# Two edits in the first front of a two-layer decoder trunk: the pace of the U gathers, and an output projection in plain f32

## The chip, the cores and the metric

One core of one Trainium2 chip runs the whole program. The time is device time of one execution in microseconds (us); the kernel before took 3003.43 us, the median of three runs (2999.48 to 3004.02). Everything is float32 in and out.

## The reference

The input is 512 tokens of 1024 features. Layer 0 mixes tokens by attention, layer 1 by a gated convolution, and each is followed by an expert retrieval (PEER):

```
for i in range(2):
    h = rmsnorm(x, norm_mix[i])
    x = x + (attention(h) if i == 0 else short_gated_conv(h))
    h = rmsnorm(x, norm_ffn[i])
    x = x + peer_ffn(h, w_query[i], sub_keys[i], u[i], v[i])
```

The attention has 16 query heads and 4 key heads of 64, a window of 128 keys, a sink per head, and ends in the output projection `o @ w_o` (1024 x 1024). The PEER step scores 2 x 128 sub-keys in each of 8 heads, takes the best 16 of the pairs per head, and so gives each token 128 of 16384 experts: `a = u[idx] . x`, `w = softmax(g) * gelu(a)`, `y = sum w * v[idx]`.

## The kernel before, in words

The tokens are four tiles of 128. The expert step is done in two ways. For tiles 2 and 3 it is **dense** (`dense`): all 16384 experts pass in 128 steps of 128 rows; each step streams one 512 KB piece of U (transposed) and one of V from HBM, splits both into a high and a low float32r part, and multiplies three products of them. For tiles 0 and 1 it is **gathered** (`gather`): 128 indirect DMAs by POOL fetch one U row per token each (`ug`, line 631, 512 KB each), VectorE multiplies each with the normed token and sums it (line 634); after the last, ScalarE's gelu and VectorE make the weights, which TensorE transposes, and 128 further gathers fetch V rows (`vg`, line 662), which TensorE multiplies in pairs (line 672). The gathered tiles share six buffers of the tag `gat`. Tile 0 and tile 1 of layer 0 follow one another in this chain, then tile 0 and tile 1 of layer 1: 1024 gathers in all.

Three generators are merged into one program order (`merge`). `stream_d` goes through the stages: attention and router of tile 0, then the **first front** (attention of tiles 1 to 3 and their router), the dense stage of layer 0, a second front (convolution of tiles 1 to 3 and their router), the dense stage of layer 1. `stream_g` is the chain of gathers, `stream_f` the small steps of tiles 0 and 1 in between. Each `yield` gives a length in the planner's own units, and the stream with the smallest sum goes on. In the first front the QKV part has 12 yields of 3.0 for all three tiles, the attention 4 yields of 6.0 per tile, the projection 8 of 10.5, the router of tiles 1 to 3 another 133 units: 36 + 72 + 84 + 133 = 325. `stream_g` waits after each gather for `rate()`: 1.3 units during the router of tile 0, and in the first front `FR0`, whose first number is for U gathers and whose second is for V gathers; in the dense stage 2.4.

```
def rate():
    u = 0 if st.get("gu") else 1
    if st["dense"]:
        return (DR1 if "f1" in st else DR0)[u]
    if st["front"]:
        return (FR1 if "f0" in st else FR0)[u]
    return GR0
```

This order is not that of the instructions in the engines' queues. A planner goes over the program with a timeline of its own and lets each engine take the earliest in program order of what it holds ready; work that is due later fills time that it takes to be free. The V matmuls are put earlier by a number of instructions: 3000 when they come up in a front, 600 otherwise. Each engine then works through its own queue in order.

The **output projection** is `proj` (line 181 on), called at the end of `attn` and of `conv`. For each half of the columns it loads four pieces of the weights (`wpo`, tag `w`, four buffers, line 186), and for each tile multiplies two 128-row slices per piece into a PSUM bank per tile (tag `y`, four banks). With `sp` given, each piece is first split: ScalarE casts it to float32r (`woh`, line 191), VectorE subtracts (`wol`, line 192), and three matmuls replace one: high x high, high x low, low x high (lines 198 to 200). The splits of the attention lie in the tag `sc` (four buffers), which the score tiles of the softmax use as well. The attention output is split in the same way (`oTh` line 342, `oTl` line 344). Without `sp`, one f32 matmul is issued (line 202); tile 0, whose attention is run alone, has always had this form.

Of the kernel before, what the change touches and what calls it, by code (L numbers as in the profile page):

```python
# [8 lines left out]
F32 = mybir.dt.float32  # L9
F32R = mybir.dt.float32r  # L10
# [5 lines left out]
ALU = mybir.AluOpType  # L16
# [3 lines left out]
P = 128  # L20
# [22 lines left out]
SCB = 4  # L43
# [27 lines left out]
P3 = 1  # L71
# [3 lines left out]

DR0 = (2.4, 2.4)
DR1 = (2.5, 2.5)
FR0 = (3.0, 3.0)
FR1 = (3.0, 3.0)


# [1 line left out]
def trunk(ctx: ExitStack, tc: tile.TileContext, a: dict, out: bass.AP):  # L83
    nc = tc.nc
# [39 lines left out]
    def py(name="py"):  # L124
        return ps_y.tile([P, 512], F32, name=name, tag="y")
# [7 lines left out]
    def pmm(name="pm"):  # L133
        return ps_m.tile([P, 512], F32, name=name, tag="m")

    def rstd_of(dst, ss, n):
        nc.vector.tensor_scalar(dst, ss, 1.0 / n, EPS, op0=ALU.mult, op1=ALU.add)
        nc.scalar.activation(dst, dst, AF.Sqrt)
        nc.vector.reciprocal(dst, dst)
# [105 lines left out]
    def attn(tiles, qks, pool, L):  # L245
        n = len(tiles)
        kT, vs, qkg, sink, nsink, cos, sin, mask = L
        nh = NH + NKV
        oTs = []
        sp = P3 and n > 1  # L250
        for j, t in enumerate(tiles):
            qk = qks[j]
            sq = pool.tile([P, nh, HD], F32, name="qsq", tag="qsq")
            nc.scalar.activation(sq, qk, AF.Square)
            ss = s2.tile([P, nh], F32, name="qss")
            nc.vector.tensor_reduce(ss, sq, axis=AX.X, op=ALU.add)
            r = s2.tile([P, nh], F32, name="qr")
            rstd_of(r, ss, HD)
            nc.vector.tensor_tensor(qk, qk, r.unsqueeze(2).to_broadcast([P, nh, HD]), op=ALU.mult)
            nc.vector.tensor_tensor(qk, qk, qkg, op=ALU.mult)  # L260
            cb = cos[:, t:t + 1, :].to_broadcast([P, nh, RH])
            sbb = sin[:, t:t + 1, :].to_broadcast([P, nh, RH])
            x1 = qk[:, :, 0:RH]
            x2 = qk[:, :, RH:2 * RH]
            rt = pool.tile([P, 4, nh, RH], F32, name="rt", tag="qsq")
            nc.vector.tensor_tensor(rt[:, 0], x1, cb, op=ALU.mult)
            nc.vector.tensor_tensor(rt[:, 1], x2, sbb, op=ALU.mult)
            nc.vector.tensor_tensor(rt[:, 2], x2, cb, op=ALU.mult)
            nc.vector.tensor_tensor(rt[:, 3], x1, sbb, op=ALU.mult)
            nc.vector.tensor_tensor(x1, rt[:, 0], rt[:, 1], op=ALU.subtract)  # L270
            nc.vector.tensor_tensor(x2, rt[:, 2], rt[:, 3], op=ALU.add)
            kd = pool.tile([P, NKV, 2, HD], F32, name="kd", tag="kd")
            nc.scalar.copy(kd, qk[:, NH:, :].unsqueeze(2).to_broadcast([P, NKV, 2, HD]))
            ps = py("psk")
            for g in range(NKV):
                nc.tensor.transpose(ps[:, g * P:(g + 1) * P], kd[:, g].rearrange("p a d -> p (a d)"), ident)
            nc.scalar.copy(kT[:, :, t * P:(t + 1) * P], ps.rearrange("p (g t) -> p g t", g=NKV))
            qT = pool.tile([P, KC, P], F32, name="qT", tag="qT")
            for half in range(2):
                ps = py("psqT")  # L280
                for k in range(4):
                    hp = half * 4 + k
                    nc.tensor.transpose(ps[:, k * P:(k + 1) * P],
                                        qk[:, 2 * hp:2 * hp + 2, :].rearrange("p a d -> p (a d)"), ident)
                nc.scalar.copy(qT[:, half * 4:half * 4 + 4, :], ps.rearrange("p (k t) -> p k t", k=4))
            if sp:
                oT = pool.tile([P, 2, 4, P], F32R, name="oTh", tag="hTa", bufs=4)
                oL = pool.tile([P, 2, 4, P], F32R, name="oTl", tag="qk", bufs=3)
            else:
                oT = oL = pool.tile([P, 2, 4, P], F32, name="oT", tag="hTa", bufs=4)  # L290
            oTs.append([(lambda k, o=o: o[:, k // 4, k % 4, :]) for o in (oT, oL)])
            if t == 0:
                k0, kw, moff, blks = 0, P, P, [0]
            else:
                k0, kw, moff, blks = (t - 1) * P, 2 * P, 0, [t - 1, t]
            nb = len(blks)
            for gp2 in range(2):
                pso = (pa, pf)[gp2]("pso")
                for gh in range(2):
                    g = gp2 * 2 + gh  # L300
                    sc = pool.tile([P, 4, 2 * P], F32, name="sc", tag="sc", bufs=SCB)
                    scv = sc[:, :, :kw]
                    psc = [py(f"psc{q}") for q in range(2)]
                    for rr in range(2):
                        for par in range(2):
                            lo = par * 64
                            nc.tensor.matmul(psc[par][:, rr * kw:(rr + 1) * kw],
                                             qT[lo:lo + 64, 2 * g + rr, :],
                                             kT[lo:lo + 64, g, k0:k0 + kw], start=True, stop=True)
                    mb = mask[:, moff:moff + kw]  # L310
                    m = s2.tile([P, 4], F32, name="m", bufs=4)
                    for r4 in range(4):
                        nc.vector.tensor_tensor_reduce(out=scv[:, r4], in0=psc[r4 % 2][:, (r4 // 2) * kw:(r4 // 2 + 1) * kw],
                                                       in1=mb, scale=0.125, scalar=GONE, op0=ALU.add, op1=ALU.max,
                                                       accum_out=m[:, r4:r4 + 1])
                    sk = sink[:, 4 * g:4 * g + 4]
                    nm = s2.tile([P, 4], F32, name="nm", bufs=4)
                    nc.vector.scalar_tensor_tensor(nm, m, -1.0, nsink[:, 4 * g:4 * g + 4],
                                                   op0=ALU.mult, op1=ALU.min)
                    es = s2.tile([P, 4], F32, name="es", bufs=4)  # L320
                    nc.vector.tensor_tensor(es, sk, nm, op=ALU.add)
                    nc.scalar.activation(es, es, AF.Exp)
                    den = s2.tile([P, 4], F32, name="den", bufs=4)
                    for r4 in range(4):
                        nc.scalar.activation(scv[:, r4], scv[:, r4], AF.Exp, bias=nm[:, r4:r4 + 1],
                                             accum_out=den[:, r4:r4 + 1])
                    nc.vector.tensor_tensor(den, den, es, op=ALU.add)
                    nc.vector.reciprocal(den, den)
                    for r4 in range(4):
                        nc.scalar.mul(scv[:, r4], scv[:, r4], den[:, r4:r4 + 1])  # L330
                    for b in range(nb):
                        psp = pmm("psp")
                        for r4 in range(4):
                            nc.tensor.transpose(psp[:, r4 * P:(r4 + 1) * P],
                                                scv[:, r4, b * P:(b + 1) * P], ident)
                        pT = pool.tile([P, 512], F32, name="pT", tag="pT", bufs=2)
                        nc.scalar.copy(pT, psp)
                        nc.tensor.matmul(pso[gh * 64:gh * 64 + 64, :], vs[:, blks[b], g * HD:(g + 1) * HD], pT,
                                         start=(b == 0), stop=(b == nb - 1))
                    yield 6.0  # L340
                psov = pso.rearrange("p (r q) -> p r q", r=4)
                nc.scalar.copy(oT[:, gp2], psov)
                if sp:
                    nc.vector.tensor_tensor(oL[:, gp2], psov, oT[:, gp2], op=ALU.subtract)
        for t in tiles:
            xs[t] = pool.tile([P, D], F32, name="x", tag="x", bufs=3)
            nc.sync.dma_start(xs[t], a["x"][t * P:(t + 1) * P, :])
        yield from proj(a["wo"], oTs, tiles, py, (pool, ("sc", "sc"), SCB) if sp else None)

    def conv(tiles, pool, psum, slow=1.0):  # L350
        n = len(tiles)
# [450 lines left out]
    def rate():  # L802
# [3 lines left out]
# [3 lines that stand above are left out]
# [179 lines left out]
```

## Time and profile before

| | |
|---|---|
| median of three runs | 3003.43 us (2999.48 to 3004.02) |
| the profiled execution | 2992.02 us |
| its span, first to last instruction | 2990.3 us |
| TensorE busy | 2626.9 us, 88% |
| VectorE busy | 2235.7 us, 75% |
| ScalarE busy | 1559.1 us, 52% |
| POOL busy | 1365.3 us, 46% |
| bytes moved | 931.38 MB, mean 311 GB/s |
| mean granted TensorE clock | 0.947 of full speed |

In the profile PE is TensorE's matmuls, PEld its weight loads, DVE VectorE, ACT ScalarE, SP the engine that issues plain DMAs. L634 is line 634 of the kernel. A name such as `ug<-in_u_dram,idx` gives the tile written and the tensors read. Times in the rows are from the span's start. The ends of matmuls are modelled and overlap, so the cost of one is read from start to start. A plain f32 matmul leaves two records, an fp32r one leaves one.

### The profile page before, as it was taken

To read this page: it belongs to the slowest core of one execution; us is meant where nothing else is said; L and a number is where in the kernel's file an instruction comes from. 1 tells how busy PE (TensorE), PEld (TensorE's weight loads), DVE (VectorE), ACT (ScalarE), POOL (GpSimd) and SP (SyncE) were. 2 spreads that over 40 slices of the span, in tenths; PEclk is the share of its full clock that TensorE was granted. 3 is DMA by queue.
4 is the path that set the end of the run, shared out by engine and by line. 5 is a ranking of instruction groups with operands and counts; after the bars stand their busy time and mean duration, and the time that the engine had idled before them with its cause. 6 is when DMAs were issued, how large, how long until landed. Compare 5 with 4: busy or idle time off the path is not lost. (4 is left out here: it accounts for less than half of the span.)

```text
span 2990.3 us, 53463 instructions
## 1 busy us (share of the span) xinstructions
PE 2626.9 (88%) x19980; PEld 2083.9 (70%) x19980; DVE 2235.7 (75%) x5234; ACT 1559.1 (52%) x2384; POOL 1365.3 (46%) x1154
## 2 busy tenths in 40 slices
PE   5974699869999889999998689997888699999998
PEld 5762368636988767777787686773677577777897
DVE  2499849888998987446699774899899957446554
ACT  4224533685673458348444333358466449547543
POOL 0157733366344455534467424236566755554000
PEclk8986799989999999999999799997999899999999
DMA  5888988989999988998999867789999998998554
GB/s 199 283 315 306 341 293 276 329 308 382 365 353 389 323 318 290 345 328 291 363 408 396 310 220 279 249 319 318 363 349 360 345 359 297 333 317 302 192 189 157
DMA packets 263204, 931.38 MB, mean 311 GB/s; under 512 B 29984, under 2 KB 38560, under 8 KB 262944
## 3 DMA queue, kind: packets, MB, share of 16 engines
q0 software_dynamic: 147456, 536.94, 49.5%
q1 hardware_dynamic: 115488, 391.03, 36.3%
q8 instruction: 157, 2.57, 0.3%
q14 instruction: 103, 0.84, 0.1%
HBM read 916.31 MB, written 11.53 MB: 310 GB/s over the span
## 5 line engine op out<-in xcount | busy, mean ns | idle before, releaser
L631 POOL DMA_INDIRECT ug<-in_u_dram,idx x512 | 668.3, 1305 | 638.1 <-DVE act L634 312.5
L662 POOL DMA_INDIRECT vg<-in_v_dram,idxT x512 | 572.2, 1118 | 689.1 <-PE acc L672 571.7
L634 DVE CUSTOM_DVE_ANT_0 ug<-ug,xn 128x1024 f32<-128x1024 f32 x512 | 622.8, 1226 | 40.3 <-DMA ug<-in_u_dram,idx 39.3
L176 PE MATMUL psA<-xh,uh 128*128 128x256 f32 x2048 | 521.1, 292 | 46.0 <-ACT uh L696 19.0
L177 PE MATMUL psA<-xl,uh 128*128 128x256 f32 x2048 | 504.2, 284 | 0.0
L176 PEld LDWEIGHTS psA<-xh,uh 128*128 128x128 f32 x2048 | 391.1, 191 | 127.9 <-ACT wh L719 32.7
L697 DVE TENSOR_TENSOR ul<-du,uh 128x1024 fp32r<-128x1024 f32 x256 | 316.6, 1237 | 181.0 <-ACT uh L696 179.1
L697 DVE TENSOR_TENSOR vl<-dv,vh 128x1024 fp32r<-128x1024 f32 x256 | 316.2, 1235 | 145.2 <-ACT vh L696 121.8
L177 PEld LDWEIGHTS psA<-xl,uh 128*128 128x128 f32 x2048 | 392.0, 191 | 4.5 <-issue 0.5
L696 ACT CAST uh<-du 128x1024 fp32r<-128x1024 f32 x256 | 268.6, 1049 | 205.3 <-PE psA L177 172.6
L696 ACT CAST vh<-dv 128x1024 fp32r<-128x1024 f32 x256 | 268.5, 1050 | 162.7 <-PE y L731 139.7
L672 PE MATMUL acc<-vg,wd 128*32 128x512 f32 x2048 | 318.1, 635 | 31.4 <-DMA vg<-in_v_dram,idxT 30.9
L731 PE MATMUL y<-vh,wh 128*128 128x512 f32 x1024 | 290.2, 406 | 34.9 <-ACT vh L696 29.9
L179 PE MATMUL psA<-xh,ul 128*128 128x256 f32 x2048 | 288.7, 283 | 10.1 <-DVE ul L697 10.0
L731 PE MATMUL y<-vl,wh 128*128 128x512 f32 x1024 | 285.7, 401 | 12.8 <-DVE vl L697 12.8
L731 PE MATMUL y<-vh,wl 128*128 128x512 f32 x1024 | 285.5, 399 | 3.0 <-DVE wl L720 3.0
L179 PEld LDWEIGHTS psA<-xh,ul 128*128 128x128 f32 x2048 | 261.8, 189 | 21.8 <-DVE ul L697 16.6
L738 ACT COPY jr<-ijg 128x2048 f16<-128x2048 f16 x128 | 243.2, 1900 | 35.0 <-DVE oj L742 33.1
L731 PEld LDWEIGHTS y<-vh,wh 128*128 128x128 f32 x1024 | 179.4, 191 | 86.5 <-ACT vh L696 36.7
L731 PEld LDWEIGHTS y<-vl,wh 128*128 128x128 f32 x1024 | 190.1, 191 | 62.9 <-DVE vl L697 18.8
L731 PEld LDWEIGHTS y<-vh,wl 128*128 128x128 f32 x1024 | 194.8, 192 | 50.9 <-DVE wl L720 4.7
L742 DVE TENSOR_TENSOR oj<-jr,io 128x2048 f16<-128x2048 f16 x128 | 157.4, 1229 | 78.0 <-PE psG L751 66.7
(208 smaller groups left out, 4021.1 us busy)
## 6 DMA issues: line engine op xcount, KB each, us to landing
du<-in_uT_dram SPq DMA_DIRECT2D x256, 512.0 KB, 6.6
dv<-in_v_dram SPq DMA_DIRECT2D x256, 512.0 KB, 5.9
wpc<-in_wq_dram SPq DMA_DIRECT2D x64, 512.0 KB, 4.8
wpc<-in_w_in_dram SPq DMA_DIRECT2D x48, 512.0 KB, 5.9
wpo<-in_wo_dram SPq DMA_DIRECT2D x16, 512.0 KB, 7.5
ug<-in_u_dram,idx POOLq DMA_INDIRECT x512
vg<-in_v_dram,idxT POOLq DMA_INDIRECT x512
wpo<-in_w_out_dram SPq DMA_DIRECT2D x16, 512.0 KB, 5.2
```

Source lines behind the costliest of these rows:

```text
L176: nc.tensor.matmul(ps, w[0][:, k, :], x[0][:, k, ts], start=(k == 0), stop=False)
L177: nc.tensor.matmul(ps, w[0][:, k, :], x[1][:, k, ts], start=False, stop=False)
L179: nc.tensor.matmul(ps, w[1][:, k, :], x[0][:, k, ts], start=False, stop=(k == KC - 1))
L631: nc.gpsimd.indirect_dma_start(out=ug, out_offset=None, in_=a[f"u{l}"], in_offset=bass.IndirectOffsetOnAxis(ap=r["idx"][h][:, c:c + 1], ax ...
L634: nc.vector.tensor_tensor_reduce(out=ug, in0=ug, in1=xn, scale=1.0, scalar=0.0, op0=ALU.mult, op1=ALU.add, accum_out=act[:, s:s + 1])
L662: ld = nc.gpsimd.indirect_dma_start(out=vg, out_offset=None, in_=a[f"v{l}"], in_offset=bass.IndirectOffsetOnAxis(ap=idxT[:, tt:tt + 1], ax ...
L672: mm = nc.tensor.matmul(acc[c:c + 32, :], wd[:, j, r8, :], vgs[j][:, h * 512:(h + 1) * 512], start=(q == 0 and r8 == 0), stop=(q == 3 and ...
L696: nc.scalar.copy(hi, w)
L697: nc.vector.tensor_tensor(lo, w, hi, op=ALU.subtract)
L731: nc.tensor.matmul(ys[tt][h], x[:, tt * P:(tt + 1) * P], m[:, h * 512:(h + 1) * 512], start=first and k == 0, stop=last and k == len(terms ...
L738: nc.scalar.copy(jr, ijg[:, 0, t0:t0 + TG].unsqueeze(2).to_broadcast([P, TG, P]))
L742: nc.vector.tensor_tensor(oj, jr, io128.unsqueeze(1).to_broadcast([P, TG, P]), op=ALU.is_equal)
```

## The change

`FR0`, the pace of the gathers in the first front, goes from 3.0 to 6.0 for U gathers and stays at 3.0 for V gathers. `attn` no longer splits anything: for tiles 1 to 3, too, the attention output is one f32 tile, and `proj` is called without `sp`. The split in `proj` stays for the convolution.

```
-FR0 = (3.0, 3.0)
+FR0 = (6.0, 3.0)
...
-        sp = P3 and n > 1
...
-            if sp:
-                oT = pool.tile([P, 2, 4, P], F32R, name="oTh", tag="hTa", bufs=4)
-                oL = pool.tile([P, 2, 4, P], F32R, name="oTl", tag="qk", bufs=3)
-            else:
-                oT = oL = pool.tile([P, 2, 4, P], F32, name="oT", tag="hTa", bufs=4)
-            oTs.append([(lambda k, o=o: o[:, k // 4, k % 4, :]) for o in (oT, oL)])
+            oT = pool.tile([P, 2, 4, P], F32, name="oT", tag="hTa", bufs=4)
+            oTs.append([lambda k, o=oT: o[:, k // 4, k % 4, :]])
...
                 nc.scalar.copy(oT[:, gp2], psov)
-                if sp:
-                    nc.vector.tensor_tensor(oL[:, gp2], psov, oT[:, gp2], op=ALU.subtract)
...
-        yield from proj(a["wo"], oTs, tiles, py, (pool, ("sc", "sc"), SCB) if sp else None)
+        yield from proj(a["wo"], oTs, tiles, py, None)
```

## Rows read from the trace of the kernel before

**Rows 1.** The page, busy tenths in 40 slices of 74.8 us each.

```profile
PE   5974699869999889999998689997888699999998
DVE  2499849888998987446699774899899957446554
```

**Rows 2.** Stretches: us; busy of PE, PEld, DVE, ACT, POOL; clock, DMA share, GB/s.

```profile
220.00:260.00 40.00, 14.45 (x48) 10.17 (x48) 38.88 (x103) 16.64 (x52) 28.36 (x24) 0.54 0.88 302
260.00:300.00 40.00, 20.87 (x88) 10.54 (x88) 39.49 (x102) 23.31 (x61) 28.89 (x24) 0.76 0.88 306
300.00:340.00 40.00, 22.14 (x92) 10.74 (x92) 38.07 (x104) 22.76 (x67) 30.23 (x25) 0.80 0.92 326
340.00:372.00 32.00, 24.68 (x76) 11.39 (x77) 27.03 (x49) 16.16 (x32) 24.07 (x20) 0.76 0.98 360
372.00:405.00 33.00, 33.00 (x166) 22.50 (x164) 11.15 (x14) 7.05 (x9) 11.49 (x12) 1.00 0.81 292
...
420.00:665.00 245.00, 208.69 (x1954) 154.80 (x1956) 209.39 (x964) 142.23 (x215) 105.98 (x99) 0.95 0.86 299
```

**Rows 3.** Groups on VectorE, 220:372: count | busy us, mean ns | idle before.

```profile
L634 DVE CUSTOM_DVE_ANT_0 ug<-ug,xn 128x1024 f32<-128x1024 f32 x90 | 108.9, 1218 | 7.5 <-DMA ug<-in_u_dram,idx 6.6
...
L634 DVE DVE_READ_ACCUMULATOR2_ANT act<- 128x1 f32 x90 | 7.4, 82 | 0.0
L344 DVE TENSOR_TENSOR oTl<-pso,oTh 128x512 fp32r<-128x512 f32 x6 | 4.1, 687 | 0.8 <-ACT oTh L342 0.8
...
L192 DVE TENSOR_TENSOR wol<-wpo,woh 128x1024 fp32r<-128x1024 f32 x3 | 3.7, 1220 | 0.0
```

**Rows 4.** Timeline of POOL: start us, us, what, idle before and its releaser.

```profile
358.58 1.99 POOL L631 DMA_INDIRECT ug<-in_u_dram,idx  x1 [0.30 <-issue]
360.87 1.44 POOL L662 DMA_INDIRECT vg<-in_v_dram,idxT  x1 [0.30 <-issue]
```

**Rows 5.** Instructions on wpo: ns min/median/max, first and last start.

```profile
L202 PEld LDWEIGHTS pswo<-wpo,oT x32: 186/190/193, 78.9 to 99.5; 128*128 128x128 f32 x32
...
L191 ACT CAST woh<-wpo x8: 1043/1048/1052, 350.2 to 393.2; 128x1024 fp32r<-128x1024 f32 x8
```

**Rows 6.** Instructions on oTh, columns as in rows 5.

```profile
L198 PEld LDWEIGHTS pswo<-woh,oTh x48: 186/188/337, 352.9 to 404.2; 128*128 128x128 f32 x48
```

**Rows 7.** Timeline of PE: start us, us (of the group, last end modelled), what.

```profile
90.19 5.32 PE L202 MATMUL pswo<-wpo,oT 128*128 128x512 f32 x12
95.35 1.28 PE L237 MATMUL psq<-wsc,hTa 128*128 128x128 f32 x10
...
403.97 0.39 PE L199 MATMUL pswo<-wol,oTh 128*128 128x512 f32 x1
...
404.88 0.39 PE L200 MATMUL pswo<-woh,oTl 128*128 128x512 f32 x1
```

**Rows 8.** Matmuls into pswo by stretch: us, PE busy, clock, DMA share, GB/s.

```profile
340.00:371.00 31.00, 7.04 (x24) 0.75 0.98 360
371.00:406.00 35.00, 28.84 (x122) 1.00 0.82 295
```

**Rows 9.** Matmuls that read vg, same columns.

```profile
371.00:406.00 35.00, 6.78 (x56) 1.00 0.82 295
```

**Rows 10.** Timeline of SP: weight pieces of the projection of tiles 1 to 3.

```profile
156.68 3.45 SPq L186 DMA_DIRECT2D wpo<-in_wo_dram  x2
...
358.64 17.82 SPq L186 DMA_DIRECT2D wpo<-in_wo_dram  x4
```

**Rows 11.** Instructions on xd, the stored token tiles, columns as in rows 5.

```profile
L686 SPq DMA_DIRECT2D xd<-xg x2: 326/326/327, 699.1 to 1466.3; - x2
...
L364 SPq DMA_DIRECT2D x<-xd x1: 424/424/424, 1645.5 to 1645.5; - x1
```

**Rows 12.** Instructions on vg, columns as in rows 5.

```profile
L662 POOL DMA_INDIRECT vg<-in_v_dram,idxT x512: 932/941/2988, 360.9 to 2775.0; - x171
```

**Rows 13.** VectorE's products of U rows, one stretch, columns as in rows 8.

```profile
1455.00:1650.00 195.00, 105.89 (x88) 1.00 1.01 396
```

**Rows 14.** The page's DMA issues: count, KB each, us to landing.

```profile
wpo<-in_wo_dram SPq DMA_DIRECT2D x16, 512.0 KB, 7.5
```

**Rows 15.** A stretch of the dense stage, columns as in rows 2.

```profile
1500.00:1575.00 75.00, 66.36 (x423) 58.77 (x422) 74.95 (x117) 31.14 (x47) 47.99 (x37) 1.00 1.03 408
```

## The prediction

> **What bounds the kernel now.** I read first the forty slices of the page [rows 1]: TensorE is at 9 nearly everywhere, but slices 3 and 4 (220 to 370 us) show it at 3 to 6 while VectorE is at 9. So the matrix engine carries the long dense stages, and the first front is one place where it doesn't. Next I cut this front into stretches [rows 2]. From 220 to 372 us the attention of tiles 1 to 3 runs: VectorE is busy 38.88, 39.49, 38.07 and 27.03 us, 143.5 of 152 us, TensorE 82.1 us at a granted clock of 0.54 to 0.80 (a mix of its levels of 1.2 and 2.4 GHz; it idles between softmax groups). From 372 to 405 TensorE is busy 33.00 of 33 us: the output projection is bound by TensorE. From 420 to 665 (router, first dense steps) TensorE has 208.7 of 245 us and VectorE 209.4, neither free.
>
> What fills VectorE in the attention is not attention. The groups of instructions in 220:372 [rows 3] show 90 products of gathered U rows, 108.9 us, with 7.4 us of reading their sums. The last U gather of the tile is issued at 358.58 and the first V gather at 360.87 [rows 4], so all 128 are through before the attention ends at about 371. By the code's paces they need not be: 31 are due before the front starts (41 units at 1.3), then one per 3.0 units; the attention ends 108 units into the front (12 x 3 for the QKV part, 12 x 6 for the groups), so 31 + 36 = 67 are due by then. The other 61 are put by the planner into VectorE time that it took to be free, though on the chip the queue is full.
>
> **A: VectorE work that goes.** The projection without split drops 8 subtractions of wol and 6 of oTl. In the attention stretch stand 3 of the former (3.7 us) and all 6 of the latter (4.1 us) [rows 3], 7.8 us in a queue that is 94% busy: 7.8 x 0.94 = 7.3, I take -7. Bounds: -7.8, and 0 if the stretch waits for gathered rows instead (DMA share 0.88 to 0.98 [rows 2]). The 8 casts on ScalarE go at no gain of their own; that engine is half idle.
>
> **B: U products due later.** At 6.0 units, 31 + 18 = 49 are due by the end of the attention, 18 fewer than 67. If the planner holds each to its due time against attention work, 18 x (1.21 + 0.08) = 23 us leave the stretch for 372 to 420, where VectorE has idle time: 33 - 11.2 us in 372 to 405 alone [rows 2]. If it fills every gap as it does now, none leave. Of the 97 products of the front, 36 are held by their due time now and 61 run ahead of it; by that share 18 x 36/97 = 6.7 leave, 8.6 us; I take -8, between 0 and -23.
>
> **C: the projection itself.** A plain f32 matmul leaves two records: 32 for the 16 of tile 0 [rows 5]. Twelve of them take from 90.19 to 95.35, 0.43 us each; an fp32r one takes 0.2275 (four from 403.97 to 404.88) [rows 7]. Removed are 144 x 0.2275 = 32.8 us, added 96 x 0.43 = 41.3: TensorE has 8.5 us more. What counts is how much is left at the end of the attention. Now 24 records are done by 371 [rows 8], and 120 x 0.2275 = 27.3 remain; with 56 V matmuls [rows 9], about 6.5 us, that fills the 34 us to 405.3. It starts so late because the first cast of weights comes at 350.2 [rows 5], though the first four weight pieces were issued by 156.68 and the next not before 358.6 [rows 10]: the casts wait for the slots that the score tiles hold. Plain f32 needs no cast. The first half of the columns of tiles 1 and 2, 32 records or 13.8 us, can go into TensorE's idle time of 300 to 340 (17.9 us) and 340 to 372 (7.3) [rows 2]; left are 27.5 us, +0.2. With tile 3's first half of these as well (8 records): 24.1, -3. If nothing starts before 353: 41.3 - 24 x 0.2275 = 35.8 against 27.3, +8.5. I take +2, 28 records done early: at the granted clock of the attention they take longer, so some won't fit.
>
> The weight loads: 190 ns f32, 188 ns fp32r [rows 5, 6], so no price. The Trainium skill (TensorE: Matmul & The Clock Gate, Weight-path perf modes) says that fast weight load is off for FP32 alone and measures about twofold; by it each of 96 loads would cost some 0.095 us more, an estimate of +9 us where not hidden. The trace disagrees: equal loads.
>
> **D: V matmuls beside the projection.** Now the first 11 V gathers are due within the front ((325 - 291)/3, with 97 x 3 = 291 of its 325 units used) and get the larger priority. Afterwards U alone reaches 43 gathers into the dense stage, so all V matmuls get the smaller one and are due later. The 56 in the projection then lie behind it or stay as fillers: 0 to -6.5, I take -3. They cost TensorE the same in the router, where 36 us of 245 are idle [rows 2]; that cover gone, they give the 3 back.
>
> **E: what the later gathers do.** Dense work starts earlier by the sum of the above, the gathers at about the same time, so the gather chain is later against it by some 16 us. The last update of tile 1 is written at 1466.3, and its reader issues at 1645.5 [rows 11]: 179 us of slack; the last gather is issued at 2775.0 [rows 12], the span ends at 2990.3. Both cover it. U products in 1455 to 1650 (88, 105.9 us [rows 13]) may lose eight (16 us at 2.2 us each) to the second front, up to -10; the V work that comes into the first dense steps may cost as much, +10. I take 0. POOL issues the same 1024 gathers in the same order; on SP the wpo loads come later, as a piece's slot is freed by its matmuls and no longer by its split, but two pieces (2 x 12 records x 0.43 = 10.3 us) cover a landing of 7.5 us [rows 14].
>
> Sum: -7 - 8 + 2 - 3 + 0 = -16 us. The profiled execution took 2992.0 (span 2990.3), 11.4 below the median of 3003.4; I carry the difference over: 2976 in such an execution, **2987** for the median. Its own range: 2970 to 2997.
>
> **How far the transfers allow it.** The stretch 220 to 372 moved 40 x (302 + 306 + 326) + 32 x 360 GB/s, 48.9 MB [rows 2]. At the 408 GB/s that 1500 to 1575 reached [rows 15] this takes 120 us, so up to 32 us could go. The Trainium skill (DMA: Bandwidth & Descriptors, Where 436 GB/s comes from) lets HBM bind at about 358 GB/s per core; by that the stretch needs 136.5 us, A and B are capped at -15.5, which would close R3 below. The trace disagrees: 408.
>
> **Rivals.**
> R1, slower: the projection's TensorE time decides. The planner puts f32 matmuls no earlier than now, and the U products take the freed VectorE slots, as they took every other slot, so the attention stays as long. Then only C's far end is left: +8.5, 3012. It decides when only some 13 records (24 x 0.2275/0.43) are done by the end of the attention, where the forecast has 28. For: TensorE is full in 372 to 405. Against: the early weights lie ready.
> R2, no change: attention bound by gathers (share 0.88 to 0.98), A and B nothing, V matmuls stay as fillers, C +2: 3005. For: 61 of 97 products run ahead of their due time anyway, and the density in 260 to 340 is that of 220 to 260 [rows 2].
> R3, far faster: A -7.8, B -23, C -3, D -6.5, E -10: -50, 2953. For: VectorE is full; against: the planner's filling.
> R4, much slower: products are held so far back that V of tile 0 starts near 665 instead of 361, 304 us later. Beyond the 179 us of slack, conv of tiles 1 to 3 waits for tile 1: +125 less what the front gains, at most 70 (its 152 us down to TensorE's 82): +55 or more, 3058. Against: products already run far ahead of their due times.
>
> **Chances.** Forecast 0.43, R3 0.12, R2 0.20, R1 0.20, R4 0.05. What a measurement can tell from no change is 0.2%, 6 us. Faster: the forecast and R3, less 0.01 at their edge, 0.54. Same: R2 and that edge, 0.21. Slower: 0.25. The range runs from just above R3, 2956, to past R1, 3015.
>
> **What would show it.** A and B: VectorE busy in the attention of tiles 1 to 3 falls from 143 us and the stretch to about 137; some 7 U products stand after it. C: pswo records start before 345, and the time from the last pso matmul to the last pswo matmul is 30 to 36 us. D: fewer than 56 vg matmuls there. E: the dense stage keeps its some 980 us (665 to 1645 now). Wrong: the attention stretch as long as before, the projection longer by 8, or xd of tile 1 written after its reader could start.

## The result, and the profile after

| | before | after |
|---|---|---|
| median | 3001.47 us (2999.48 to 3004.02, 4 runs) | 3045.05 us (3042.06 to 3050.79, 4 runs) |
| profiled execution, its span | 2992.02, 2990.3 us | 3042.06, 3040.3 us |
| mean granted clock | 0.947 | 0.936 |

The change costs 1.47% (ratio 1.0147, interval 1.0129 to 1.0165): slower, and outside the range that was predicted. Lines of the kernel after have other numbers: 624 is the U gather (631 before), 627 its product (634), 655 the V gather (662), 724 the dense stage's second matmul (731), 679 the store of a gathered tile (686), 357 its reader (364).

The page comes first, forty slices of 76 us; they answer to [rows 1].

```profile
PE   5973889869999989999994698986998689999998
DVE  2499748986997997456552999997489998446455
```

The first front still shows its dip (slices 3 and 4 read 3 and 8 now, 4 and 6 before). New are a 4 and a 6 of TensorE at slices 21 and 22, which begin 1596 us into the span, and the lean stretch of VectorE in the slices before, which read 4, 5, 6, 5, 5 and then 2 in slice 21. The hole is more than a millisecond away from both edits.

To place it, I read first and last starts by tile. `y` is what the dense stage sums up, `psbcu` the convolution of tiles 1 to 3. Of before and then after, columns as in rows 5:

```profile
L731 PE MATMUL y<-vl,wh x512: 387/390/792, 679.1 to 1644.2; 128*128 128x512 f32 x171
...
L176 PE MATMUL psbcu<-hh,whi x192: 335/336/659, 1674.5 to 1788.8; 128*128 128x384 f32 x192
```

```profile
L724 PE MATMUL y<-vl,wh x512: 387/389/793, 681.3 to 1595.7; 128*128 128x512 f32 x171
...
L176 PE MATMUL psbcu<-hh,whi x192: 333/336/686, 1704.5 to 1814.2; 128*128 128x384 f32 x192
```

The same reading at every stage boundary gives the whole 50.0 us between the two spans (the medians lie 43.6 us apart; the profiled execution of before was faster than its median):

| stage | before | after | difference |
|---|---|---|---|
| start to the first y of dense stage 0 | 672.3 | 670.8 | -1.5 |
| dense stage 0, first to last y | 971.9 | 924.9 | -47.0 |
| last y to the first matmul of the convolution | 30.3 | 108.8 | **+78.5** |
| convolution, to its last projection matmul | 158.3 | 145.6 | -12.7 |
| router, to its last score matmul | 129.2 | 126.2 | -3.0 |
| to the first y of dense stage 1 | 129.9 | 153.1 | +23.2 |
| dense stage 1 | 886.0 | 898.4 | +12.4 |
| to the end of the span | 12.4 | 12.5 | +0.1 |

**The first front** hardly moved: 1.5 us where 16 were forecast. Its stretches after, which answer to [rows 2]:

```profile
220.00:260.00 40.00, 13.90 (x48) 9.65 (x48) 38.87 (x105) 16.14 (x49) 28.44 (x25) 0.54 0.87 305
260.00:300.00 40.00, 20.39 (x88) 10.45 (x88) 39.36 (x103) 24.33 (x64) 28.66 (x25) 0.76 0.90 316
300.00:340.00 40.00, 32.38 (x116) 15.21 (x116) 37.58 (x103) 22.38 (x66) 30.41 (x26) 0.90 0.92 321
340.00:372.00 32.00, 24.31 (x62) 9.34 (x62) 23.28 (x46) 13.05 (x28) 22.12 (x20) 0.79 0.99 372
372.00:405.00 33.00, 31.68 (x100) 11.68 (x99) 6.05 (x11) 6.46 (x10) 6.54 (x7) 1.00 0.70 238
420.00:665.00 245.00, 213.04 (x1944) 155.11 (x1940) 208.38 (x966) 142.05 (x213) 99.02 (x96) 0.93 0.83 292
```

VectorE is as full as it was up to 340, though the four `oTl` subtractions that stood there are gone (before, they start at 278.5, 290.3, 322.9 and 334.7), and TensorE has ten more busy microseconds in 300 to 340: the plain f32 matmuls, early. The group of the U products there, which answers to the first of [rows 3], and POOL's timeline, which answers to [rows 4]:

```profile
L627 DVE CUSTOM_DVE_ANT_0 ug<-ug,xn 128x1024 f32<-128x1024 f32 x91 | 110.2, 1219 | 7.1 <-DMA ug<-in_u_dram,idx 6.2
```

```profile
358.54 0.97 POOL L624 DMA_INDIRECT ug<-in_u_dram,idx  x1 [0.30 <-issue]
359.81 0.96 POOL L655 DMA_INDIRECT vg<-in_v_dram,idxT  x1 [0.30 <-issue]
...
1417.85 1.45 POOL L706 TENSOR_TENSOR dw<-dw,G 128x256 f32<-128x256 f32 x1 [3.05 <-issue]
...
1596.85 0.97 POOL L655 DMA_INDIRECT vg<-in_v_dram,idxT  x1 [177.56 <-DVE cc L397]
1598.13 1.11 POOL L655 DMA_INDIRECT vg<-in_v_dram,idxT  x1 [0.31 <-issue]
1609.20 0.94 POOL L655 DMA_INDIRECT vg<-in_v_dram,idxT  x1 [9.96 <-PE acc L665]
...
1651.99 0.93 POOL L655 DMA_INDIRECT vg<-in_v_dram,idxT  x1 [0.30 <-issue]
1653.22 0.93 POOL L624 DMA_INDIRECT ug<-in_u_dram,idx  x1 [0.30 <-PE acc L665]
```

The pace of the U gathers was halved, and yet 91 products stand where 90 stood, and the last U gather goes out at 358.54 instead of 358.58. The pace puts the gathers into the program order; the planner takes them out of it again and fills the front as before.

The rest of the same timeline is the hole. From 1419.3 POOL stands for 177.6 us in front of one V gather of tile 1, and goes on at 1596.85, when the dense stage is through. In before the last V gather of tile 1 had been served in time for a store at 1466.3 [rows 11]. What POOL waits for shows on the other engines: VectorE's timeline, then ScalarE's, around the last dense matmul (1595.7).

```profile
1592.00 0.42 DVE L713 TENSOR_TENSOR wl<-dw,wh 128x256 fp32r<-128x256 f32 x1
1596.12 0.17 DVE L397 COPY cc<-zh 128x2 f32<-128x2 f32 x1 [3.71 <-PE y L724]
```

```profile
1596.12 1.99 ACT L170 CAST whi<-wpc 128x1024 fp32r<-128x1024 f32 x2 [4.99 <-PE y L724]
```

These are the first writes into tiles of the second front's memory (pool `f1`), and each of them is released by the last `y`. That memory is what the dense stage's pool gives back. The view puts the gather's release down to the copy into `cc`; that the gather, too, waited for the dense stage to give its memory back is read from the code, and the experiments put it on trial. V gathers of tile 1 were given buffers from that pool:

```
        with tc.tile_pool(name="dn", bufs=1) as dn:
            yield from dense(0, r, dn)
...
        with tc.tile_pool(name="f1", bufs=1) as f1:
            if GX1:
                st["gx"] = (f1, "gx", GX1)
            finish(0, st["ys"], f1)
            yield "g0_1"
...
    def gtile(name):
        x = st.get("gx")
        if x:
            gcount[0] = (gcount[0] + 1) % (GAT + x[2])
            if gcount[0] >= GAT:
                return x[0].tile([P, D], F32, name=name, tag=x[1], bufs=x[2])
        return gp.tile([P, D], F32, name=name, tag="gat")
```

`GAT` is 6 and `GX1` is 2; `yield "g0_1"` holds this stream until tile 1's chain has come up to its end. Of eight gathers that come up after the dense stage in the program order, six take a buffer of `gat` and two one of `f1`. The planner may move a gather ahead, but one that writes into `f1` can't run before the dense stage has ended, and POOL works its queue in order, so all that stand behind it in the queue wait too. By the paces, 42.8 U gathers of tile 0 are left when the dense stage begins (128 - 31 - 325/6), and 384 more follow for V of tile 0 and U and V of tile 1: 427 x 2.4 = 1024 units, and the dense stage has 912.6 (128 x 6.8 + 15 + 16 x 1.7). So some 47 gathers of tile 1 come up behind it. In before it was 116.7 + 256 gathers, 894.5 units: all inside, with 18 units to spare.

By the counter in `gtile`, the first five of the 47 take `gat`, the next two `f1`, and the six after them `gat` again. The trace fits that to the gather. After the stop come two gathers, and then a pause of 9.96 us that ends with a V matmul, as no buffer was free. Matmuls that read V rows on TensorE from there, columns as in rows 8:

```profile
1600.00:1720.00 120.00, 35.90 (x168) 0.60 0.94 356
```

One gather leaves four matmul records (2048 for 512 gathers), so 42 gathers are multiplied after the stop, though POOL issues only 36 of them there. The other six had been moved ahead of the two that wait, and their rows lay unread in the buffers of `gat`. 5 + 6 + 36 makes the 47.

While POOL stands, the dense stage has the chip to itself. This row of after answers to [rows 15], and the products of U rows in two stretches to [rows 13]:

```profile
1500.00:1575.00 75.00, 75.00 (x484) 68.15 (x484) 41.46 (x54) 36.27 (x54) 0.00 (x0) 1.00 0.57 188
```

```profile
1455.00:1650.00 195.00, 0.00 (x0) 0.90 0.62 218
...
1705.00:1976.00 271.00, 120.14 (x100) 0.95 0.90 331
```

TensorE is busy for all 75 us (66.4 before), at 188 GB/s instead of 408, and the stage ends 48.5 us early. But the 88 products of tile 0's second layer that ran in 1455 to 1650 before [rows 13] are put off: the second front now holds 100 of them, against 29 in before, and behind it stand the V gathers (73 against 61 in the stretch up to the first y of dense stage 1). The row of before:

```profile
1675.00:1962.00 287.00, 35.23 (x29) 0.98 0.72 247
```

I put the +23.2 and the +12.4 of the table down to that; no run separates it from other causes. What the runs show is that dense stage 1 takes 898 to 911 us in the four kernels with a hole and 885 to 894 in the eight without.

After the stop, POOL has 36 V gathers left, and the convolution waits for what they give. SP's timeline of after, the store and its reader, answers to [rows 11]:

```profile
1664.43 0.33 SPq L679 DMA_DIRECT2D xd<-xg  x1
1670.86 0.33 SPq L357 DMA_DIRECT2D x<-xd  x1
```

Stretches of the hole, columns as in rows 2:

```profile
1596.00:1645.00 49.00, 24.95 (x121) 3.98 (x120) 5.19 (x8) 1.99 (x2) 29.39 (x32) 0.66 0.88 331
1645.00:1704.00 59.00, 16.25 (x74) 5.89 (x71) 40.01 (x69) 9.91 (x19) 46.16 (x41) 0.53 0.99 382
```

TensorE is busy 41.2 of 108 us, and 35.9 of them are V matmuls, in step with the gathers (36 from 1596.85 to 1651.99, one per 1.58 us).

### The profile page after: what moved, and what is told of

Same layout as the page of the kernel before. It is cut to its first block, busy times and chain, and to the rows that moved or that the text cites. A ratio compares the mean times of both kernels' runs of the same rounds, so it can differ in the third digit from the quotient of the medians.

```text
span 3040.3 us, 53338 instructions
## 1 busy us (share of the span) xinstructions
PE 2633.9 (87%) x19932; PEld 2074.7 (68%) x19932; DVE 2222.7 (73%) x5212; ACT 1546.6 (51%) x2374; POOL 1366.2 (45%) x1162
## 3 DMA queue, kind: packets, MB, share of 16 engines
q0 software_dynamic: 147456, 536.94, 48.5%
## 4 chain that ended last, share of the span: by engine, by line
PE 42%; DVE 7%; issue 6%; DMA 4%; POOL 3%; ACT 1%; POOLq 0%; DVEq 0%; ACTq 0%
PE y L724 16%; PE psA L176 5%; PE acc L665 5%; PE psA L179 5%; PE psA L177 5%; DMA vg<-in_v_dram,idxT 3%; POOL ug L624 3%; DVE ug L627 2%; PE psG L744 1%; DMA ug<-in_u_dram,idx 1%; DVE ul L690 1%; PE psbcu L176 1%; PE psbcu L177 1%; PE psbcu L179 1%; PE psrq L556 1%
## 5 line engine op out<-in xcount | busy, mean ns | idle before, releaser
L655 POOL DMA_INDIRECT vg<-in_v_dram,idxT x512 | 558.1, 1090 | 802.6 <-PE acc L665 510.9
L176 PEld LDWEIGHTS psA<-xh,uh 128*128 128x128 f32 x2048 | 388.8, 190 | 128.9 <-ACT wh L712 42.8
```

What stands on the lines that cost most here:

```text
L176: nc.tensor.matmul(ps, w[0][:, k, :], x[0][:, k, ts], start=(k == 0), stop=False)
L655: ld = nc.gpsimd.indirect_dma_start(out=vg, out_offset=None, in_=a[f"v{l}"], in_offset=bass.IndirectOffsetOnAxis(ap=idxT[:, tt:tt + 1], ax ...
```

## The experiments

The theory on trial: the hole comes from gathers that stand behind the dense stage in the program order and take buffers that the dense stage still holds. Its rivals: the projection in plain f32 makes it, or the later place of the gathers alone does (they are due later, so they run later, whatever their buffers). `before` is measured again in each group of runs: 2999.66 us (22 runs) beside the first four, 2998.33 (19) beside the next four, 2998.25 (19) beside the last two.

**e1_pace**: the kernel before with one edit.

```
-FR0 = (3.0, 3.0)
+FR0 = (6.0, 3.0)
```

> The pace alone (U gathers of the first front at 6.0), the split projection kept. Theory 1 (buffers): of the V gathers of tile 1, 47 come up behind the dense stage of layer 0 in program order; there two gathers in eight take buffers of a pool that has memory only after the dense stage, so POOL, which works in order, stops at the first of them: the hole at 1600 to 1700 us is there, 3045 us (3035 to 3055). Theory 2 (the f32 projection delays the chain): no hole, 3003 us.

Measured: 3053.16 us (3052.36 to 3058.25, 4 runs), ratio 1.0183 (1.0156 to 1.0211). The last y starts at 1595.7 and the first matmul of the convolution at 1704.6, as in after. V gathers on POOL in two stretches, columns as in rows 8 with POOL's busy time in place of TensorE's:

```profile
1390.00:1590.00 200.00, 0.00 (x0) 1.00 0.55 179
1590.00:1660.00 70.00, 34.06 (x36) 0.70 0.83 321
```

The pace alone makes the hole, to the same 36 gathers. The projection has no part in it.

**e2_proj**: the kernel after with the pace back at 3.0, so the projection in plain f32 alone.

```
-FR0 = (6.0, 3.0)
+FR0 = (3.0, 3.0)
```

> The f32 projection alone, the pace back at 3.0. Theory 1: no hole, every V gather of tile 1 before 1480 us, 2995 to 3008 us, as TensorE's 8.5 us more are mostly covered. Theory 2: the hole, 3045 us.

Measured: 3013.89 us (3001.64 to 3017.69, 8 runs), ratio 1.0051 (1.0035 to 1.0066). Last y 1645.2, first matmul of the convolution 1675.6: no hole. Plain f32 alone is half a per cent slower, 6 us above the window that I gave for the theory on trial (2995 to 3008): right about the hole, a miss on the time. Its profiled execution is the fastest of its runs, 12 us below their median, so its trace can't say where those go.

**e3_gxlate**: the kernel after, and the extra buffers are opened behind the wait for the chain. The gathers stay where they are in the program order and in their due times; only their buffers change.

```
-            if GX1:
-                st["gx"] = (f1, "gx", GX1)
             finish(0, st["ys"], f1)
             yield "g0_1"
+            if GX1:
+                st["gx"] = (f1, "gx", GX1)
```

> Both edits, and the two extra gather buffers of the second front are handed out only to gathers that come up after tile 1 of layer 0 is through. Theory 1: the V gathers of tile 1 run on through the dense stage, no hole, 2985 to 3005 us. Theory 3 (their late place in program order alone holds them back): the hole stays, 3040 to 3050 us.

Measured: 2986.91 us (2981.92 to 2997.54, 10 runs), ratio 0.997 (0.9954 to 0.9985). Instructions on `xd`, and the first matmul of the convolution:

```profile
L679 SPq DMA_DIRECT2D xd<-xg x2: 326/326/327, 734.8 to 1484.4; - x2
...
L357 SPq DMA_DIRECT2D x<-xd x1: 424/424/424, 1636.9 to 1636.9; - x1
```

```profile
L176 PE MATMUL psbcu<-hh,whi x192: 336/336/658, 1664.8 to 1766.9; 128*128 128x384 f32 x192
```

The hole is gone. The store comes at 1484.4, 18 us later than before (the later due times do show), and still 152 us ahead of its reader. So the later place alone costs no hole, and the buffers are needed for one.

**e4_dr0**: the kernel after with a shorter pace in the dense stage, so that the whole chain comes up inside it: 427 x 2.1 = 896 units of 912.6.

```
-DR0 = (2.4, 2.4)
+DR0 = (2.1, 2.1)
```

> Both edits, and the gathers in the dense stage of layer 0 at 2.1 units instead of 2.4, so that all of them come up inside it (43 x 2.1 + 384 x 2.1 = 897 of 912 units). Theories 1 and 3: no hole, 2990 to 3008 us. Theory 2: the hole, 3045 us.

Measured: 3005.52 us (3001.97 to 3013.68, 10 runs), ratio 1.0021 (1.0005 to 1.0036). Last y 1644.2, first matmul of the convolution 1679.2: no hole, though the extra buffers are opened as early as in after. The place in the order is the other half of the cause.

**e5_slowv**: the kernel before, neither edit, with slower V gathers in the dense stage: 116.7 x 3 + 128 x 2.4 + 128 x 3 = 1041 units, so that 43 come up behind it.

```
-DR0 = (2.4, 2.4)
+DR0 = (2.4, 3.0)
```

> The kernel before, with neither edit, and the V gathers in the dense stage of layer 0 at 3.0 units instead of 2.4: 117 x 3.0 + 128 x 2.4 + 128 x 3.0 = 1042 of 912 units, so 43 V gathers of tile 1 come up behind the dense stage. Theory 1: POOL stops at the first that needs one of the two extra buffers, some 33 to 43 gathers are left for a hole of 80 to 100 us after the dense stage, 3040 to 3060 us. Rival (the hole needs the edits of the change): no hole, 3000 us.

Measured: 3044.57 us (3042.01 to 3050.93, 4 runs), ratio 1.0161 (1.0142 to 1.0181). POOL's timeline:

```profile
1598.69 0.98 POOL L662 DMA_INDIRECT vg<-in_v_dram,idxT  x1 [238.95 <-DVE cc L404]
```

The same stop, 239 us long, and gone 1.2 us after the last y of this kernel starts (1597.5); 32 gathers are issued from there on, where I had said 33 to 43. The hole needs neither of the two edits, only gathers behind the dense stage.

**e7_fr4**: the kernel after with the pace at 4.0: (15.75 + 384) x 2.4 = 959 units, 20 behind the dense stage.

```
-FR0 = (6.0, 3.0)
+FR0 = (4.0, 3.0)
```

> Both edits, the pace of U gathers at 4.0 instead of 6.0: 16 U gathers reach into the dense stage, (16 + 384) x 2.4 = 960 of 912 units, so some 20 V gathers of tile 1 come up behind it. Theory 1: the hole shrinks with their number to about half, 3015 to 3035 us. Rival (any gather left behind costs the whole hole): 3045 us.

Measured: 3032.47 us (3031.44 to 3036.64, 4 runs), ratio 1.0113 (1.0096 to 1.0129). POOL's timeline, and V gathers in the stretch from there:

```profile
1625.67 0.94 POOL L655 DMA_INDIRECT vg<-in_v_dram,idxT  x1 [160.07 <-DVE cc L397]
```

```profile
1622.00:1700.00 78.00, 8.21 (x8) 0.59 0.87 330
```

A smaller hole with fewer gathers, though its price, 1.13%, is three quarters of the 1.47% of after. The four kernels that have it, side by side:

| | behind the dense stage by the paces | V gathers issued after the stop | V gathers multiplied after it | last y to store | store to first convolution matmul |
|---|---|---|---|---|---|
| after | 47 | 36 | 42 | 68.7 us | 40.1 us |
| e1_pace | 47 | 36 | 42 | 68.9 | 40.0 |
| e5_slowv | 43 | 32 | 38 | 61.0 | 39.7 |
| e7_fr4 | 20 | 8 | 14 | 30.9 | 39.9 |

In each of the four, six more gathers are multiplied after the stop than issued (168, 168, 152 and 56 records). With the five that passed this gives 47, 47, 43 and 19, the numbers of the paces. So a hole is 40 us from the store to the convolution, about 31 us for eight gathers and what comes with them, and, by an estimate from after and e7_fr4, 1.35 us for each further one ((68.7 - 30.9)/28). Before, with no gather left, has 30.3 us between the last y and the convolution. Against that e7_fr4, at 70.8 us, pays 40.5 for its eight gathers, and after pays 78.5 for its 36. Carried back from eight to none at 1.35 each, some 30 us of either price stay, however few gathers are left; no run here had fewer than eight.

**e8_pacegx**: the edit of e1_pace and that of e3_gxlate on the kernel before; the projection stays split.

```
-FR0 = (3.0, 3.0)
+FR0 = (6.0, 3.0)
...
-            if GX1:
-                st["gx"] = (f1, "gx", GX1)
             finish(0, st["ys"], f1)
             yield "g0_1"
+            if GX1:
+                st["gx"] = (f1, "gx", GX1)
```

> The pace at 6.0, the extra buffers handed out after tile 1, and the split projection kept. If the f32 projection costs what it cost alone (some 10 us), this is 2970 to 2982 us and the fastest; if with the pace it costs nothing, 2985 to 2992 us like both edits with late buffers.

Measured: 3003.26 us (2995.75 to 3007.66, 11 runs), ratio 1.0013 (1 to 1.0025). The hole is gone (last y 1643.1, convolution 1675.7), but the time is in neither of the windows that I gave: a miss. The gain of e3_gxlate over before isn't there with the split projection.

**e9_fr12gx**: e8_pacegx with the pace at 12.0.

```
-FR0 = (6.0, 3.0)
+FR0 = (12.0, 3.0)
```

> As the run before with the pace at 12.0 instead of 6.0. If the pace doesn't govern when a U gather of the first front is executed (the planner fills what is free), the 128 U gathers of tile 0 still end before 372 us and the first y product of the dense stage stays within 666 to 674 us, and the time is within 0.5% of the run before. If it does govern, U gathers of tile 0 move behind 372 us and the front gets shorter.

Measured: 2990.21 us (2979.91 to 2995.0, 8 runs), ratio 0.9967 (0.9952 to 0.9982). U gathers on POOL up to the dense stage:

```profile
100.00:372.00 272.00, 151.50 (x128) 0.81 0.91 322
372.00:660.00 288.00, 0.00 (x0) 0.92 0.82 286
```

All 128 U gathers of tile 0 go out by 372 at a quarter of the pace too, as in every kernel here. The pace doesn't govern the front.

**e10_gxonly**: the moved line of e3_gxlate alone, on the kernel before.

```
-            if GX1:
-                st["gx"] = (f1, "gx", GX1)
...
             yield "g0_1"
+            if GX1:
+                st["gx"] = (f1, "gx", GX1)
```

> The kernel before (U pace 3.0, split kept), with only the one line moved: the extra gather buffers are opened after the wait for tile 1's gather chain instead of before it. Before, no gather of tile 1's first layer stood behind the dense stage, so nothing can wait there. Buffers as the cause of the hole: same as before, 2995 to 3007, first convolution matmul 25 to 35 us after the last dense y. If the moved line is worth something on its own (so that the gain of e3_gxlate over before came from it and not from the two edits): 2978 to 2992, the 12 to 15 us of e3_gxlate.

Measured: 2998.8 us (2996.24 to 3000.64, 10 runs), ratio 0.9999 (0.999 to 1.0009). No gather stands behind the dense stage there, and the line does nothing by itself. So what it gave in e3_gxlate is the hole, and no gift of its own.

**e11_f32fr12**: e3_gxlate with the pace at 12.0.

```
-FR0 = (6.0, 3.0)
+FR0 = (12.0, 3.0)
```

> Both edits with the buffers opened late, and the pace of U gathers in the first front at 12.0. With the pace doing nothing to the front itself (e9_fr12gx), only the re-planned order moves the time: 2980 to 2997. If the gains of e3_gxlate and e9_fr12gx over before (12 and 8 us) have separate causes and add up: 2973 to 2980. If a still later chain holds up the convolution after all: over 3005, with over 60 us from last y to first convolution matmul.

Measured: 2999.95 us (2995.79 to 3005.18, 10 runs), ratio 1.0008 (0.9998 to 1.0018). No hole (1650.3 to 1680.6), but the time lies in none of the windows that I gave: a miss. The gains don't add up.

With the line moved, the five kernels read 2999 (split, pace 3), 3003 (split, 6), 2990 (split, 12), 2987 (f32, 6) and 3000 (f32, 12). Going from 6 to 12 gains 13 us with the split and loses 13 without. Each differs from the others by the planner's whole order after the front, and I could not put these steps of 0.3 to 0.4% down to one place: that stays open. e3_gxlate and e9_fr12gx beat the kernel before by 0.3%, and neither edit can be credited with it.

## Why the prediction was wrong

It was wrong in its direction, and its 2987 lies 58 us below the median after. One step decides that; the sum for the front was wrong as well.

**E failed**: "Both cover it. I take 0". The shift is about as large as forecast, 18 us (the store at 1484.4 in e3_gxlate against 1466.3) for 16, but by luck: the dense stage was to start earlier, and it starts within 1.5 us of where it did, while the chain itself runs later. The cover was real: e3_gxlate has the shift and 152 us of slack left, at no cost. What the step left out is that a slack in time is not all that a gather needs. It also needs a buffer, and which buffer it gets is settled by its place in the program order, where the margin was 18 planner units, not 179 us. The change overran that margin: POOL stood for 177.6 us, and the convolution started 78.5 us later behind the dense stage. The term E was put at 0; its sign of being wrong, `xd` of tile 1 written after its reader could start, came true at 1664.4. I worked out that 43 U gathers would reach into the dense stage (D), and didn't carry the sum on to the other end of that stage, 427 x 2.4 against 912.6. The code that opens the buffers ahead of the wait lay more than 500 lines behind the diff, outside of the functions that it touches.

**R4** named the right place, convolution of tiles 1 to 3 waiting for tile 1, at 3058, and got 0.05. Its condition (V of tile 0 starts near 665) didn't come true: the first V gather went out at 359.81. "Products already run far ahead of their due times" was true of the front, and no evidence on a gather whose memory isn't there yet.

**B failed**: -8 was taken, and 0 came. All 128 U gathers are out by 358.54, and the last attention matmul of tiles 1 to 3 comes 8.4 us later, not earlier. The bound of 0 in that step ("if it fills every gap as it does now, none leave") is what happened, and it did so too in e9_fr12gx at a quarter of the pace.

**A** came to little: VectorE is busy 139.1 us in 220 to 372 against 143.5 (sum of the stretches above and of [rows 2]), but the attention didn't end earlier, since TensorE was now in its way. Its timeline after, near the end of the attention, and ScalarE's copy that gave the last two matmuls their input:

```profile
372.50 5.32 PE L202 MATMUL pswo<-wpo,oT 128*128 128x512 f32 x12
377.75 1.07 PE L333 MATMUL pso<-pT,vs 128*64 128x512 f32 x2
```

```profile
372.14 0.59 ACT L332 COPY pT<-psp 128x512 f32<-128x512 f32 x1 [0.18 <-PE psp L329]
```

The input was there at 372.7; twelve projection records, 5.3 us, lie in TensorE's queue ahead of the last two of the attention. That is 5.0 of the 8.4 us; the rest I did not place. Work that was put into idle time early also stands in front of what the path needs.

**C** was right in its mechanism: matmuls into `pswo` start at 328.2 instead of 353.0, and these rows answer to [rows 8].

```profile
300.00:341.00 41.00, 11.11 (x26) 0.91 0.92 322
341.00:371.00 30.00, 6.89 (x16) 0.77 0.99 372
371.00:406.00 35.00, 25.00 (x56) 1.00 0.71 248
```

Two records straddle 341 and count in both rows: 40 of 96 are done by 371 where I had counted on 28 (in the same way the 24 of before were 22, as 122 of 144 stand in 371 to 406). The projection ends at 400.7, 4.2 us earlier; A to D together had said 16. By the prediction's own measure, from the last attention matmul to the last one of the projection, it takes 22.5 us instead of 35.1, outside of the 30 to 36 that were to show C: 12.6 less where C and D had said 1. **D**: 40 V matmuls are left in 371 to 406, of 56 [rows 9]. They cost 5.95 us instead of 6.78, so 0.8 of that went, not 3.

The sum for the front was -16, and -1.5 came: +8.4 to the end of the attention, -12.6 in the projection, +2.7 from there to the first y. In e3_gxlate it is +0.5 (first y at 672.8). So the forecast would not have been right without the hole either: e3_gxlate, the change without it, is 13 us faster than before and ends at the 2987 that was forecast, but by luck, since none of it comes from the front, and e8_pacegx and e11_f32fr12 show how little that number holds. R1's mechanism didn't occur (the projection started and ended earlier), though plain f32 alone costs 0.5% by e2_proj, a price that I found no place for. R2 was right that A and B bring nothing. R3 had nothing to build on.

## What to carry to other kernels

Before you call a shift covered by slack, ask of each shifted instruction not only when its reader comes but where its buffer comes from, and whether it still stands on the same side of the point where a pool closes or a flag switches buffers; count that margin in the units that set the order. In an engine's queue that runs in order, one instruction whose memory is still held stops everything behind it, ready or not, and the price does not shrink in proportion to the work that is left: eight gathers left over made 70.8 us between the two stages, 36 made 108.8, and none 30.3. And where a planner fills gaps by itself, changing a pace changes the program order and not the stretch it is named for: look at what the order does at its far end.

## What the runs showed of the hardware

Issuing a gather cost POOL less where VectorE was quiet. In after, groups on POOL in 1380 to 1660, where VectorE hardly works after 1596, and then in 1660 to 1704, where it multiplies U rows:

```profile
L655 POOL DMA_INDIRECT vg<-in_v_dram,idxT x36 | 33.9, 943 | 198.6 <-DVE cc L397 177.6 <-PE acc L665 13.3 <-issue 7.8
...
L624 POOL DMA_INDIRECT ug<-in_u_dram,idx x6 | 5.6, 937 | 2.1 <-issue 1.2 <-PE acc L665 0.8
```

```profile
L624 POOL DMA_INDIRECT ug<-in_u_dram,idx x29 | 35.9, 1236 | 8.8 <-issue 8.1 <-PE acc L665 0.4 <-DMA ug<-in_u_dram,idx 0.3
```

The mean is 943 ns against 1236, and it is not V rows against U rows: the six U gathers of the first stretch, which start before VectorE's first product (1660.05), take 937. The Trainium skill (SBUF — State Buffer, "SBUF: two separate sides") says that a VectorE instruction with two SBUF inputs and a GpSimd instruction that reads SBUF take turns on one pair of ports, whole instructions at a time. A product of a gathered row with the token has two such inputs, and the two means fit the rule if issuing a gather counts as reading SBUF (its row numbers lie in the tile `idx`); no run here shows that it does, or separates it from other causes.

The granted clock fell with the hole: 1.00, the level of 2.4 GHz, in the dense row of 1500 to 1575, then 0.66 and 0.53, mostly that of 1.2 GHz, while TensorE was busy 25 of 49 and then 16 of 59 us.
